# A streaming encoder step: 32 frames of the fifth dense tile move from the all-expert path to gathered rows

## The chip, the core and the metric

One core of a Trainium2 chip runs the whole program. The metric is the device time of one execution in microseconds (us), the median of several runs. TensorE is called PE here (PEld is its weight load), VectorE is DVE, ScalarE is ACT, GpSimd is POOL, and SP is the queue from which most DMAs are issued.

## What is computed

One layer over 1,024 prompt frames and 32 sample frames of width 1,024: an input projection, a differential attention and a recurrent branch, an output projection, and then PEER, a layer of 16,384 single-neuron experts, followed by a last RMSNorm. The change touches PEER and that norm alone:

```python
q = (xs @ w_q).reshape(P_TBLOCK, P_HEADS, 2, P_DQ)
s = einsum('thcd,hckd->thck', q, sub_keys)
sv, si = top_k(s, 16)                              # per half key
cv, ci = top_k(comb, 16)                           # 16 experts of each of 8 heads
e = ...                                            # 128 expert numbers of a frame
gate = softmax(cv)
hid = gelu(einsum('thkd,td->thk', down[e], xs))
out = einsum('thkd,thk->td', up[e], gate * hid)
h = h + out;  y = rmsnorm(h, final_norm)
```

Each frame uses 128 of the 16,384 experts.

## The kernel before

The frames lie in tiles of 128: prompt tiles 0 to 7, and tile S with the 32 sample frames. Five generators (`gemm`, `attn`, `routing`, `scatter`, `rows`) are interleaved by costs that the code gives them; the framework then fixes one order of instructions for each engine when the program is built.

PEER has two forms. **The dense form** (tiles 0 to 4, `DENSE`, together `NV` = 640 frames) sends every frame through all experts. The experts stand as 128 columns of 128. For a column `e`, `hidden(e)` multiplies all frames by the column's down weights (two halves of 320 frames, 24 matmuls each, since each float product is made of three float32r ones) and applies gelu. `gated(e)` multiplies by a gate matrix that is zero nearly everywhere and splits the product into a high and a low part (`vwh`, `vwl`, `WR` = 6 buffers each). Four columns make a block: 32 of them. In a block, the loop over `db` multiplies by the up weights and DVE adds the result to `acc` (L1274). A block has 384 matmuls, half of them of `hidden` for the block that follows. The weights come by `dr` and `ur` (8 loads of 256 KB of each per block).

The gate matrix is made by `scatter()`: four frames at a time, ACT, DVE and POOL build one-hot rows, `grid` multiplies them on PE and evicts them into `stg` (one buffer); every 16 frames one store of 1 MB goes to `W_d` in HBM, from which `gated` loads it (`gw`). The dense stage begins only when all gates are stored. Until then `v_start` makes the first `GE` = 6 columns of gelu values and keeps them in `early`.

**The row form** (`ROWS` = 5, 6, S, 7) gathers. For each of a frame's 128 experts, POOL issues an indirect DMA (L1044) that brings 128 rows of 8 KB (down and up) into one of `RB` = 5 buffers; DVE makes the dot product (L1047, an accumulating multiply), ACT gelu and gate (L1049, L1050), and DVE adds the weighted up row to an accumulator in PSUM (L1031). Only then is the buffer free. Tile S has 32 frames, so its 128 experts are laid in four runs of 32 over the partitions: 32 gathers serve it. At its end the four runs are folded together (L1066 to L1071). Each tile ends with `normed` (L1004) and takes row buffers for that too. That makes 3 x 128 + 32 = 416 gathers.

`routing()` makes the lists (`topk`) on DVE; those of tiles 5, 6, S and 7 are made while the dense stage runs. Work of `rows` is held back in the order of DVE so that it runs at most 60 us of its own cost account ahead of `gemm`.

Of the kernel before, what the change touches and what calls it, by code (L numbers as in the profile page):

```python
# [17 lines left out]
DEC = 32  # L18
# [11 lines left out]
CDG = [[0, 1, 2], [3, 4], [5, 6, 7, "S"]]  # L30

DENSE = [0, 1, 2, 3, 4]
ROWS = [5, 6, "S", 7]
RORDER = [0, 1, 2, 3, 4, 5, 6, 7, "S"]

DEFER = [6, 7]
# [6 lines left out]

PRE = [2, 1]

RB, VR, VB, BB, OHB = 5, 3, 2, 4, 4

CSH = 2

GX = (3, 6, 3)  # L50

GE = 6

GC, SC = 1.65, 1.0

# [4 lines left out]

def rows_of(t):
    return DEC if t == "S" else 128


@with_exitstack
def step_kernel(ctx, tc, x_prompt, x_sample, cache_kT, cache_v, state, norm1, w_in, lam_params,
# [4 lines left out]
    V, A, PE, G, SP = nc.vector, nc.scalar, nc.tensor, nc.gpsimd, nc.sync  # L71
# [46 lines left out]
    ident = consts.tile([128, 128], F32, name="ident")  # L118
# [160 lines left out]
    def halves(x):  # L279
        return x[:, 0:4], x[:, 4:8]  # L280
# [637 lines left out]
    def topk(t):  # L918
        pk, twk = P["pk"], P["twk"]
        T = rows_of(t)  # L920
# [7 lines left out]
        for h0 in range(0, PH, hg):  # L928
# [54 lines left out]
            V.tensor_copy(out=e3[:T, h0:h0 + hg], in_=ef[:T])  # L983
            HEADS[t] = h0 + hg
            yield 1.0
        if t == "S":

            es = pk.tile([128, 32], I32, name="es", tag="es")
            gs = pk.tile([128, 32], F32, name="gts", tag="gts")
            for g in range(4):  # L990
                SP.dma_start(out=es[g * 32:(g + 1) * 32], in_=ei[:32, g * 32:(g + 1) * 32])
                SP.dma_start(out=gs[g * 32:(g + 1) * 32], in_=gate[:32, g * 32:(g + 1) * 32])
            ei, gate = es, gs
        ROUTE[t] = ROUTING[t] = (gate, ei)
        yield 3.0


    def normed(pool, ht, fnb, t, sq):

        T = rows_of(t)  # L1000
        ss = pool.tile([128, 1], F32, name="ssf", tag="ssf", bufs=2)
        A.activation(sq[:T], ht[:T], AF.Square, accum_out=ss[:T])
        r = rstd_of(pool, ss, 1, D, T, tag="f")
        V.scalar_tensor_tensor(out=sq[:T], in0=ht[:T], scalar=r[:T], in1=fnb[:T],  # L1004
                               op0=OP.mult, op1=OP.mult)
        SP.dma_start(out=y_sample if t == "S" else y_prompt[t * 128:t * 128 + 128, :], in_=sq[:T])

    def rows():

        for t in ROWS:  # L1010
            while t not in ROUTING or "gat" not in P:
                yield None
            gate, ei = ROUTING[t]
            T = rows_of(t)
            nk = 32 if t == "S" else 128
            gat = P["gat"]

            def wide(name):
                return gat.tile([128, 2 * D], F32, name=name, tag="row", bufs=RB)

            xt = gat.tile([128, D], F32, name="xg", tag="xg", bufs=1)
            for g in range(128 // T):
                SP.dma_start(out=xt[g * T:(g + 1) * T], in_=xn_d[t][:, :])
            hid = gat.tile([128, 128], F32, name="hid", tag="hid", bufs=1)
            acc = P["xgp"].tile([128, D], F32, name="xp", tag="xp")

            def add(k, row):
                if k == 0 and t == "S":
                    V.tensor_scalar(acc, row[:, D:], hid[:, 0:1], None, op0=OP.mult)
                else:  # L1030
                    V.scalar_tensor_tensor(out=acc, in0=row[:, D:], scalar=hid[:, k:k + 1],  # L1031
                                           in1=acc if k else first, op0=OP.mult, op1=OP.add)

            first = None
            if t != "S":
                first = wide("first")[:, 0:D]
                SP.dma_start(out=first, in_=h1_d[t][:, :])

            late = []
            for k in range(nk):  # L1040
                while t not in ROUTE and HEADS.get(t, 0) * 16 <= k:
                    yield None
                row = wide("row")
                G.indirect_dma_start(out=row, out_offset=None, in_=p_rows,  # L1044
                                     in_offset=bass.IndirectOffsetOnAxis(ap=ei[:, k:k + 1], axis=0))
                h = hid[:, k:k + 1]
                V.tensor_tensor_reduce(out=row[:, 0:D], in0=row[:, 0:D], in1=xt, scale=1.0, scalar=0.0,  # L1047
                                       op0=OP.mult, op1=OP.add, accum_out=h)
# [12 lines left out]
            ht = acc  # L1061
            if t == "S":

                ht = hw[:, 0:D]
                SP.dma_start(out=ht[:T], in_=h1_d[t][:, :])
                V.tensor_copy(out=full, in_=acc)  # L1066
                pw = wide("runs")
                V.tensor_add(ht[:T], ht[:T], acc[:T])
                for g, part in enumerate((pw[:, 0:D], pw[:, D:], sq)):
                    SP.dma_start(out=part[:T], in_=full[(g + 1) * T:(g + 2) * T])  # L1070
                    V.tensor_add(ht[:T], ht[:T], part[:T])  # L1071
            normed(gat, ht, fnb, t, sq)
            yield 4.0


    NV = 128 * len(DENSE)
    SB = 16
    W_d = dram([128 // JB, 128, NV // SB, JB, SB], "W_d")

# [10 lines left out]
    def grid(t, s0, q, stg, am, bm):  # L1090
        ps = ws_bank()
        for u in range(4):
            PE.matmul(ps[:, u * 128:(u + 1) * 128], am[:, u], bm[:, u], start=True, stop=True)  # L1093
        A.activation(stg[:, :, :, q:q + 4],
                     ps.rearrange("p (t b j) -> p b j t", t=4, j=JB), AF.Copy)
        if q + 4 == SB:
            o = (128 * DENSE.index(t) + s0) // SB
            SP.dma_start(out=W_d[:, :, o].rearrange("b i j t -> i b j t"), in_=stg)

    def scatter():  # L1100

        late = None
        for t in [x for ts in CDG for x in ts if x in DENSE]:
# [13 lines left out]
            A.activation(tr[:, 0:3], ps.rearrange("p (a t) -> p a t", a=4)[:, 0:3], AF.Copy)  # L1117
            A.activation(tr[:, 3], ps[:, 0:128], AF.Copy, scale=-1.0)

            for s0 in range(0, 128, SB):  # L1120
                stg = sct.tile([128, 128 // JB, JB, SB], F32, name="stg", tag="stg", bufs=1)
                for q in range(0, SB, 4):
                    pool, bufs = (P["oh"], OHB) if "oh" in P else (sct, 2)
# [19 lines left out]
            late = None  # L1143
            DONE.add(t)

    JU, WR = 4, 6
    NCH = -(-NV // 512)
    CHUNK = NV // NCH
    CS = [slice(j * CHUNK, (j + 1) * CHUNK) for j in range(NCH)]
# [22 lines left out]
    def v_start():  # L1172


        VX["early"] = P["vk"].tile([128, KD, NV], F32, name="early", tag="acc")
        xh = VX["xh"] = P["vx"].tile([128, KD, NV], F32R, name="vxh")
        xl = VX["xl"] = P["vx"].tile([128, KD, NV], F32R, name="vxl")

        places = [(t, i) for t in range(len(DENSE)) for i in range(2)]
        half = len(places) // 2  # L1180
        xs = []
        for h in range(2):
            x = P["gw"].tile([128, half, 512], F32, name="vxs", tag="gw", bufs=2)
            for j, (t, i) in enumerate(places[h * half:(h + 1) * half]):
                SP.dma_start(out=x[:, j], in_=xn_d[DENSE[t]][:, i * 512:(i + 1) * 512])
                xs.append(x[:, j])
        for (t, i), x in zip(places, xs):
            transposed_half(gv_bank, x, 128, halves(xh)[i], halves(xl)[i], 128 * t)
            yield 1.0
        for e in range(GE):  # L1190
            hidden(e)
            yield 3 * KD * NV / 2400.

    def stage_v():
        n = NV
        with tc.tile_pool(name="v_wk", bufs=2) as wk:
# [32 lines left out]
            def residual(d0):  # L1229

                cs = slice(d0 * 128, d0 * 128 + 512)
                for i in range(len(DENSE)):
                    ps = gv_bank()
                    for d in range(4):
                        PE.transpose(ps[:, d * 128:(d + 1) * 128],
                                     acc[:, d0 + d, i * 128:(i + 1) * 128], ident)
                    V.tensor_add(ht[:, i, cs], ht[:, i, cs], ps)
                    A.activation(sq[:, i, cs], ht[:, i, cs], AF.Square,
                                 accum_out=s2[:, d0 // 4, i:i + 1])
                    G.tensor_tensor(out=ht[:, i, cs], in0=ht[:, i, cs], in1=fnb[:, cs], op=OP.mult)  # L1240

            for jb in range(NJ):
                if jb == NJ - 1:
# [2 lines left out]
                    fnb = P["gw"].tile([128, D], F32, name="fnb", tag="gw", bufs=2)  # L1246
                    s2 = wk.tile([128, 2, len(DENSE)], F32, name="s2", tag="s2", bufs=1)
                    ss = wk.tile([128, len(DENSE)], F32, name="ss", tag="ss", bufs=1)
                    late = [(ht[:, i], h1_d[t][:, :]) for i, t in enumerate(DENSE)]
                    late.append((fnb, row_bcast(final_norm)))  # L1250
                for dq in range(4):
                    if jb + 1 < NJ:
# [25 lines left out]

            r = rstd_of(wk, ss, len(DENSE), D, tag="v")
            for i, t in enumerate(DENSE):  # L1280
                V.tensor_scalar(sq[:, i], ht[:, i], r[:, i:i + 1], None, op0=OP.mult)
                SP.dma_start(out=y_prompt[t * 128:t * 128 + 128, :], in_=sq[:, i])
            yield 10.0

    STATE = set()
# [162 lines left out]
```

## Time and profile before

| | |
|---|---|
| median of 3 runs | 3603.99 us (3594.76 to 3604.02) |
| the profiled execution | 3604.3 us |
| its span | 3602.5 us |
| PE, PEld busy | 3259.8 us (90%), 3135.7 us (87%) |
| DVE busy | 2834.6 us (79%) |
| POOL, ACT busy | 2018.5 us (56%), 1614.2 us (45%) |
| mean granted clock of PE | 0.952 |
| DMA | 881.01 MB, mean 245 GB/s |

Busy time is the union of the instructions' times on an engine, and matmuls are pipelined: the spacing of their starts tells their cost, not their duration. What an engine waited for is inferred from semaphores. The granted clock is 1.00 at 2.4 GHz and 0.50 at 1.2 GHz.

### The profile page before, as it was taken

What the parts mean: (1) busy time and instruction counts of PE and PEld (TensorE: products, weight loads), DVE (VectorE), ACT (ScalarE), POOL (GpSimd) and SP (SyncE); (2) the same over time, 40 slices, a digit from 0 to 9 for tenths busy, and PEclk for the clock granted to TensorE, in tenths of its full rate; (3) what the DMA queues carried; (4) which work ended last, traced back from release to release, by engine and by line L of the source; (5) the groups of instructions that cost most, each with busy time, mean ns of one, the idle gap of its engine ahead of it and who ended that gap; (6) DMA issues with size and microseconds to landing.
All of it is one profiled execution on the core that took longest, in us unless ns stands there. A gap on an engine that the chain in (4) does not pass through costs nothing.

```text
span 3602.5 us, 60487 instructions
## 1 busy us (share of the span) xinstructions
PE 3259.8 (90%) x21635; PEld 3135.7 (87%) x21635; DVE 2834.6 (79%) x6148; ACT 1614.2 (45%) x4034; POOL 2018.5 (56%) x1339
## 2 busy tenths in 40 slices
PE   7999899989988888774899888999999999999997
PEld 6989899877877887774899888999999999999997
DVE  3354468898678999988999999888888888788833
ACT  3544344456777747763333333333333333333322
POOL 2322224546334556565666569666766676677633
PEclk9999999999988999886999999999999999999999
DMA  4554364444565635489888778999889898999832
GB/s 163 167 159 149 109 206 167 158 138 149 173 191 161 227 123 153 139 321 343 307 318 323 299 269 312 356 338 359 314 324 355 300 355 324 346 336 351 298 109 94
DMA packets 357453, 881.01 MB, mean 245 GB/s; under 512 B 31008, under 2 KB 190240, under 8 KB 299808
## 3 DMA queue, kind: packets, MB, share of 16 engines
q1 hardware_dynamic: 297248, 440.91, 36.9%
q0 software_dynamic: 59904, 436.23, 31.8%
q8 instruction: 171, 2.80, 0.3%
q14 instruction: 130, 1.06, 0.1%
HBM read 784.47 MB, written 92.14 MB: 243 GB/s over the span
## 4 chain that ended last, share of the span: by engine, by line
PE 57%; DVE 28%; DMA 4%; issue 4%; ACT 3%; POOL 2%; SPq 0%; DVEq 0%; ACTq 0%; POOLq 0%
PE gv L261 12%; PE gv L262 11%; PE gv L263 11%; PE gm L261 6%; PE gm L263 6%; PE gm L262 6%; DVE row L1047 5%; DVE xp L1031 5%; DVE acc L1274 2%; DVE oh L967 2%; PE ws L1093 1%; DVE ohB L1132 1%; DVE ef L972 1%; PE gb L468 1%; DMA row<-in_p_rows_dram,ei 1%
## 5 line engine op out<-in xcount | busy, mean ns | idle before, releaser
L261 PE MATMUL gv<-vwh,uh 128*128 128x320 f32 x2048 | 648.3, 317 | 96.7 <-DVE acc L1274 63.9
L255 POOL TENSOR_TENSOR wl<-wr,wh 128x1024 fp32r<-128x1024 f32 x160 | 390.4, 2453 | 540.7 <-ACT wh L254 524.9
L261 PE MATMUL gv<-vxh,dh 128*128 128x320 f32 x2048 | 643.9, 315 | 21.7 <-DVE acc L1274 10.2
L1044 POOL DMA_INDIRECT row<-in_p_rows_dram,ei x384 | 514.3, 1339 | 259.1 <-DVE xp L1031 141.7
L263 PE MATMUL gv<-vxh,dl 128*128 128x320 f32 x2048 | 639.8, 313 | 8.7 <-POOL dl L255 8.7
L262 PE MATMUL gv<-vwl,uh 128*128 128x320 f32 x2048 | 640.8, 313 | 0.0
L262 PE MATMUL gv<-vxl,dh 128*128 128x320 f32 x2048 | 639.7, 313 | 0.0
L263 PE MATMUL gv<-vwh,ul 128*128 128x320 f32 x2048 | 638.3, 313 | 0.5 <-POOL ul L255 0.5
L1047 DVE CUSTOM_DVE_ANT_0 row<-row,xg 128x1024 f32<-128x1024 f32 x416 | 599.4, 1441 | 3.1 <-DMA row<-in_p_rows_dram,ei 2.1
L1031 DVE SCALAR_TENSOR_TENSOR xp<-row,hid,xp 128x1024 f32<-128x1024 f32 x412 | 528.4, 1283 | 78.8 <-ACT hid L1050 77.0
L261 PEld LDWEIGHTS gv<-vwh,uh 128*128 128x128 f32 x2048 | 391.9, 191 | 111.6 <-DVE acc L1274 76.7
L255 POOL TENSOR_TENSOR dl<-dr,dh 128x512 fp32r<-128x512 f32 x256 | 361.3, 1415 | 201.4 <-ACT dh L254 193.4
L255 POOL TENSOR_TENSOR ul<-ur,uh 128x512 fp32r<-128x512 f32 x256 | 368.0, 1438 | 181.6 <-ACT uh L254 162.3
L261 PEld LDWEIGHTS gv<-vxh,dh 128*128 128x128 f32 x2048 | 392.0, 191 | 28.2 <-DVE vwl L255 13.1
L263 PEld LDWEIGHTS gv<-vxh,dl 128*128 128x128 f32 x2048 | 391.5, 191 | 9.5 <-POOL dl L255 9.5
L262 PEld LDWEIGHTS gv<-vwl,uh 128*128 128x128 f32 x2048 | 392.5, 192 | 0.0
L263 PEld LDWEIGHTS gv<-vwh,ul 128*128 128x128 f32 x2048 | 391.5, 192 | 0.9 <-POOL ul L255 0.9
L262 PEld LDWEIGHTS gv<-vxl,dh 128*128 128x128 f32 x2048 | 392.1, 191 | 0.0
L1135 POOL TENSOR_TENSOR ohB<-ohB,tr 128x512 f32<-128x512 f32 x160 | 200.0, 1256 | 262.4 <-DVE ohB L1132 216.8
L1274 DVE TENSOR_TENSOR acc<-acc,gv 128x320 f32<-128x320 f32 x496 | 235.4, 479 | 93.5 <-PE gv L263 90.2
L1049 ACT ACTIVATE hid<-hid 128x1 f32<-128x1 f32 x416 | 82.9, 199 | 486.5 <-DVE hid L1047 482.1
L254 ACT ACTIVATE uh<-ur 128x512 fp32r<-128x512 f32 x256 | 161.2, 630 | 301.3 <-PE gv L262 209.3
(324 smaller groups left out, 7520.7 us busy)
## 6 DMA issues: line engine op xcount, KB each, us to landing
dr<-in_p_downT_dram SPq DMA_DIRECT2D x256, 256.0 KB
ur<-in_p_up_dram SPq DMA_DIRECT2D x256, 256.0 KB
wr<-in_w_in_dram SPq DMA_DIRECT2D x88, 512.0 KB
W_d<-stg SPq DMA_DIRECT2D x40, 1024.0 KB
gw<-W_d SPq DMA_DIRECT2D x32, 1280.0 KB
wr<-in_p_wq_dram SPq DMA_DIRECT2D x48, 512.0 KB
wr<-in_w_out_dram SPq DMA_DIRECT2D x24, 512.0 KB
wr<-in_w_a_dram SPq DMA_DIRECT2D x12, 512.0 KB
```

What stands on the lines that cost most here:

```text
L254: A.activation(h, src, AF.Copy)
L255: (lo_engine or G).tensor_tensor(out=l, in0=src, in1=h.bitcast(F32), op=OP.subtract)
L261: PE.matmul(out, lh, rh, start=(i == 0), stop=False)
L262: PE.matmul(out, lh, rl, start=False, stop=False)
L263: PE.matmul(out, ll, rh, start=False, stop=(i == n - 1))
L967: V.tensor_tensor(out=oh[:T], in0=cf[:T, h].unsqueeze(2).to_broadcast([T, 16, NCAND]), in1=iota_c[:T].unsqueeze(1).to_broadcast([T, 16, NC ...
L1031: V.scalar_tensor_tensor(out=acc, in0=row[:, D:], scalar=hid[:, k:k + 1], in1=acc if k else first, op0=OP.mult, op1=OP.add)
L1044: G.indirect_dma_start(out=row, out_offset=None, in_=p_rows, in_offset=bass.IndirectOffsetOnAxis(ap=ei[:, k:k + 1], axis=0))
L1047: V.tensor_tensor_reduce(out=row[:, 0:D], in0=row[:, 0:D], in1=xt, scale=1.0, scalar=0.0, op0=OP.mult, op1=OP.add, accum_out=h)
L1049: A.activation(h, h, AF.Gelu)
L1135: G.tensor_tensor(out=bm, in0=bm, op=OP.mult, in1=tr[:, 2, xs].unsqueeze(2).to_broadcast([128, 4, 128]))
L1274: V.tensor_add(acc[:, db, cs], acc[:, db, cs], ps[:, :CHUNK])
```

## The change

Tile 4 is cut: its first 96 frames stay dense, and its last 32 become a row tile "4b" that is handled as S is, ahead of tile 5. The dense form then has 608 frames in two halves of 304, and the scatter of tile 4 ends after 96 frames. There are 448 gathers. `GE` goes from 6 to 8, `WR` from 6 to 8, and `RB` from 5 to 4. The dense norm's reads and writes shrink to the frames that are there.

```diff
 DENSE = [0, 1, 2, 3, 4]
-ROWS = [5, 6, "S", 7]
+CUT = {4: 96}
+ROWS = ["4b", 5, 6, "S", 7]
-RB, VR, VB, BB, OHB = 5, 3, 2, 4, 4
+RB, VR, VB, BB, OHB = 4, 3, 2, 4, 4
-GE = 6
+GE = 8
+def dense_of(t):
+    return CUT.get(t, 128)
...
-        if t == "S":
-            es = pk.tile([128, 32], I32, name="es", tag="es")
-            gs = pk.tile([128, 32], F32, name="gts", tag="gts")
+        if t == "S" or t in CUT:
+            es = pk.tile([128, 32], I32, name="es", tag="es", bufs=2)
+            gs = pk.tile([128, 32], F32, name="gts", tag="gts", bufs=2)
+            o = CUT.get(t, 0)
             for g in range(4):
-                SP.dma_start(out=es[g * 32:(g + 1) * 32], in_=ei[:32, g * 32:(g + 1) * 32])
+                SP.dma_start(out=es[g * 32:(g + 1) * 32], in_=ei[o:o + 32, g * 32:(g + 1) * 32])
...
+            small = t in ("S", "4b")
+            T, of, o = (DEC, 4, CUT[4]) if t == "4b" else (rows_of(t), t, 0)
+            nk = 32 if small else 128
...
-    NV = 128 * len(DENSE)
+    VT = [dense_of(t) for t in DENSE]
+    VO = [sum(VT[:i]) for i in range(len(VT))]
+    NV = sum(VT)
...
-            for s0 in range(0, 128, SB):
+            for s0 in range(0, dense_of(t), SB):
...
-    JU, WR = 4, 6
+    JU, WR = 4, 8
...
-                for i in range(len(DENSE)):
+                for i, (o, T) in enumerate(zip(VO, VT)):
...
+                    V.memset(s2, 1.0)
```

## Rows read from the trace of the kernel before

**Rows 1.** Busy time by stretch: length, PE, PEld, DVE, ACT, POOL; clock; DMA share; GB/s.
```profile
1500.00:1630.00 130.00, 97.50 (x602) 93.05 (x601) 116.55 (x246) 89.50 (x244) 87.70 (x68) 0.84 0.86 304
1630.00:1680.00 50.00, 5.98 (x34) 5.48 (x33) 37.34 (x53) 15.09 (x50) 22.90 (x16) 0.57 0.97 369
1680.00:2290.00 610.00, 546.07 (x3473) 535.96 (x3474) 597.03 (x1272) 214.23 (x572) 424.99 (x296) 0.93 0.84 309
2290.00:3425.00 1135.00, 1112.87 (x7504) 1103.21 (x7503) 941.64 (x1426) 422.92 (x1142) 783.83 (x565) 1.00 0.89 332
3425.00:3603.00 178.00, 156.12 (x1068) 154.82 (x1066) 62.13 (x131) 46.43 (x99) 64.30 (x50) 0.95 0.30 102
```

**Rows 2.** The same view for line L1031 alone: DVE's additions of gathered rows.
```profile
1500.00:1680.00 180.00, 42.17 (x32) 0.77 0.89 322
1680.00:2290.00 610.00, 161.81 (x127) 0.93 0.84 309
2290.00:3425.00 1135.00, 330.32 (x257) 1.00 0.89 332
```

**Rows 3.** Timeline of PE, starts in us: nine of 320 columns, eight of 256.
```profile
2304.80 0.31 PE L261 MATMUL gv<-vxh,dh 128*128 128x320 f32 x1
...
2305.97 0.31 PE L263 MATMUL gv<-vxh,dl 128*128 128x320 f32 x1
...
1011.77 0.28 PE L262 MATMUL gm<-act,wh 128*128 128x256 f32 x1
...
1012.59 0.28 PE L263 MATMUL gm<-act,wl 128*128 128x256 f32 x1
```

**Rows 4.** Groups of instructions: one of six dense groups (busy, mean ns, idle before).
```profile
L261 PE MATMUL gv<-vxh,dh 128*128 128x320 f32 x2048 | 643.9, 315 | 21.7 <-DVE acc L1274 10.2 <-DVE vwl L255 8.6 <-DVE vxl L272 1.9
```

**Rows 5.** The chain that ended last, 1630 to 1682 us: start, length, what.
```profile
1630.70 16.81 DMA W_d<-stg
...
1652.93 1.29 DVE xp L1031
...
1662.00 1.29 DVE xp L1031
...
1678.25 3.48 DVE early L1211 x6
```

**Rows 6.** Stores of the gate matrix, 1500 to 1720 us: count, first and last issue.
```profile
L1098 SPq DMA_DIRECT2D W_d<-stg x8: 370/377/392, 1505.5 to 1652.7; - x8
```

**Rows 7.** Groups of DVE's instructions, 2300 to 3400 us.
```profile
L1047 DVE CUSTOM_DVE_ANT_0 row<-row,xg 128x1024 f32<-128x1024 f32 x249 | 345.5, 1388 | 1.0 <-DMA row<-in_p_rows_dram,es 0.8
L1031 DVE SCALAR_TENSOR_TENSOR xp<-row,hid,xp 128x1024 f32<-128x1024 f32 x247 | 317.7, 1286 | 61.7 <-ACT hid L1050 60.8 <-ACT hid L1049 0.5 <-issue 0.2
```

**Rows 8.** Waits of POOL, 2300 to 3400 us: us in total, times, longest.
```profile
POOL row L1044 <- DVE xp L1031: 85.0, 82, 4.1
```

**Rows 9.** The page's DMA queue of the gathers, and issues with their sizes.
```profile
q0 software_dynamic: 59904, 436.23, 31.8%
...
dr<-in_p_downT_dram SPq DMA_DIRECT2D x256, 256.0 KB
ur<-in_p_up_dram SPq DMA_DIRECT2D x256, 256.0 KB
...
gw<-W_d SPq DMA_DIRECT2D x32, 1280.0 KB
```

**Rows 10.** Timeline of DVE: last row of tile S, first row of tile 7.
```profile
2847.72 1.22 DVE L1047 CUSTOM_DVE_ANT_0 row<-row,xg 128x1024 f32<-128x1024 f32 x1
...
2869.04 1.23 DVE L1047 CUSTOM_DVE_ANT_0 row<-row,xg 128x1024 f32<-128x1024 f32 x1
```

**Rows 11.** Timeline of DVE: the last gathered row, its norm, the last dense addition.
```profile
3421.30 1.22 DVE L1047 CUSTOM_DVE_ANT_0 row<-row,xg 128x1024 f32<-128x1024 f32 x1
...
3430.56 1.27 DVE L1004 SCALAR_TENSOR_TENSOR ht<-xp,rsf,fnb 128x1024 f32<-128x1024 f32 x1
...
3581.58 0.49 DVE L1274 TENSOR_TENSOR acc<-acc,gv 128x320 f32<-128x320 f32 x1 [1.27 <-PE gv L263]
```

More of the change, by code (lines that the diff above doesn't have):

```diff
@@ L985, in topk, with normed @@
             yield 1.0
-        if t == "S":
-            es = pk.tile([128, 32], I32, name="es", tag="es")
-            gs = pk.tile([128, 32], F32, name="gts", tag="gts")
+        if t == "S" or t in CUT:
+            es = pk.tile([128, 32], I32, name="es", tag="es", bufs=2)
+            gs = pk.tile([128, 32], F32, name="gts", tag="gts", bufs=2)
+            o = CUT.get(t, 0)
             for g in range(4):
-                SP.dma_start(out=es[g * 32:(g + 1) * 32], in_=ei[:32, g * 32:(g + 1) * 32])
-                SP.dma_start(out=gs[g * 32:(g + 1) * 32], in_=gate[:32, g * 32:(g + 1) * 32])
-            ei, gate = es, gs
-        ROUTE[t] = ROUTING[t] = (gate, ei)
+                SP.dma_start(out=es[g * 32:(g + 1) * 32], in_=ei[o:o + 32, g * 32:(g + 1) * 32])
+                SP.dma_start(out=gs[g * 32:(g + 1) * 32], in_=gate[o:o + 32, g * 32:(g + 1) * 32])
+            small = "%sb" % t if t in CUT else t
+            ROUTE[small] = ROUTING[small] = (gs, es)
+        if t != "S":
+            ROUTE[t] = ROUTING[t] = (gate, ei)
         yield 3.0
-    def normed(pool, ht, fnb, t, sq):
-        T = rows_of(t)
+    def normed(pool, ht, fnb, dst, sq):
+        T = dst.shape[0]
         ss = pool.tile([128, 1], F32, name="ssf", tag="ssf", bufs=2)
@@ L1005, in normed @@
                                op0=OP.mult, op1=OP.mult)
-        SP.dma_start(out=y_sample if t == "S" else y_prompt[t * 128:t * 128 + 128, :], in_=sq[:T])
+        SP.dma_start(out=dst, in_=sq[:T])
     def rows():
@@ L1013, in rows @@
             gate, ei = ROUTING[t]
-            T = rows_of(t)
-            nk = 32 if t == "S" else 128
+            small = t in ("S", "4b")
+            T, of, o = (DEC, 4, CUT[4]) if t == "4b" else (rows_of(t), t, 0)
+            nk = 32 if small else 128
+            dst = y_sample if t == "S" else y_prompt[of * 128 + o:of * 128 + o + T, :]
             gat = P["gat"]
@@ L1022, in rows @@
             for g in range(128 // T):
-                SP.dma_start(out=xt[g * T:(g + 1) * T], in_=xn_d[t][:, :])
+                SP.dma_start(out=xt[g * T:(g + 1) * T], in_=xn_d[of][o:o + T, :])
             hid = gat.tile([128, 128], F32, name="hid", tag="hid", bufs=1)
@@ L1027, in add @@
             def add(k, row):
-                if k == 0 and t == "S":
+                if k == 0 and small:
                     V.tensor_scalar(acc, row[:, D:], hid[:, 0:1], None, op0=OP.mult)
@@ L1034, in rows @@
             first = None
-            if t != "S":
+            if not small:
                 first = wide("first")[:, 0:D]
@@ L1061, in rows @@
             ht = acc
-            if t == "S":
+            if small:
                 ht = hw[:, 0:D]
-                SP.dma_start(out=ht[:T], in_=h1_d[t][:, :])
+                SP.dma_start(out=ht[:T], in_=h1_d[of][o:o + T, :])
                 V.tensor_copy(out=full, in_=acc)
@@ L1071, in rows @@
                     V.tensor_add(ht[:T], ht[:T], part[:T])
-            normed(gat, ht, fnb, t, sq)
+            normed(gat, ht, fnb, dst, sq)
             yield 4.0
-    NV = 128 * len(DENSE)
+    VT = [dense_of(t) for t in DENSE]
+    VO = [sum(VT[:i]) for i in range(len(VT))]
+    NV = sum(VT)
     SB = 16
@@ L1096, in grid @@
         if q + 4 == SB:
-            o = (128 * DENSE.index(t) + s0) // SB
+            o = (VO[DENSE.index(t)] + s0) // SB
             SP.dma_start(out=W_d[:, :, o].rearrange("b i j t -> i b j t"), in_=stg)
@@ L1184, in v_start @@
             for j, (t, i) in enumerate(places[h * half:(h + 1) * half]):
-                SP.dma_start(out=x[:, j], in_=xn_d[DENSE[t]][:, i * 512:(i + 1) * 512])
+                SP.dma_start(out=x[:VT[t], j], in_=xn_d[DENSE[t]][:VT[t], i * 512:(i + 1) * 512])
                 xs.append(x[:, j])
         for (t, i), x in zip(places, xs):
-            transposed_half(gv_bank, x, 128, halves(xh)[i], halves(xl)[i], 128 * t)
+            transposed_half(gv_bank, x, VT[t], halves(xh)[i], halves(xl)[i], VO[t])
             yield 1.0
@@ L1231, in residual @@
                 cs = slice(d0 * 128, d0 * 128 + 512)
-                for i in range(len(DENSE)):
+                for i, (o, T) in enumerate(zip(VO, VT)):
                     ps = gv_bank()
                     for d in range(4):
[L1235 to L1240, printed above, removed]
+                        PE.transpose(ps[:T, d * 128:(d + 1) * 128], acc[:, d0 + d, o:o + T], ident)
+                    V.tensor_add(ht[:T, i, cs], ht[:T, i, cs], ps[:T])
+                    A.activation(sq[:T, i, cs], ht[:T, i, cs], AF.Square,
+                                 accum_out=s2[:T, d0 // 4, i:i + 1])
+                    G.tensor_tensor(out=ht[:T, i, cs], in0=ht[:T, i, cs], in1=fnb[:T, cs], op=OP.mult)
             for jb in range(NJ):
@@ L1248, in stage_v @@
                     ss = wk.tile([128, len(DENSE)], F32, name="ss", tag="ss", bufs=1)
-                    late = [(ht[:, i], h1_d[t][:, :]) for i, t in enumerate(DENSE)]
+                    V.memset(s2, 1.0)
+                    late = [(ht[:VT[i], i], h1_d[t][:VT[i], :]) for i, t in enumerate(DENSE)]
                     late.append((fnb, row_bcast(final_norm)))
@@ L1280, in stage_v @@
             for i, t in enumerate(DENSE):
-                V.tensor_scalar(sq[:, i], ht[:, i], r[:, i:i + 1], None, op0=OP.mult)
-                SP.dma_start(out=y_prompt[t * 128:t * 128 + 128, :], in_=sq[:, i])
+                T = VT[i]
+                V.tensor_scalar(sq[:T, i], ht[:T, i], r[:T, i:i + 1], None, op0=OP.mult)
+                SP.dma_start(out=y_prompt[t * 128:t * 128 + T, :], in_=sq[:T, i])
             yield 10.0
```

## The prediction

> **What bounds the kernel now.** I first read busy time by stretch, because the share over the whole span mixes stages. From 1500 us on there are four of them [rows 1]. Up to 1680 us the gate matrix is finished: in the last 50 us of that PE works 6 us. From 1680 to 2290 us DVE is busy 597 of 610 us: it makes the lists of the later tiles, takes gathered rows and serves the dense loop. From 2290 to 3425 us PE is busy 1112.9 of 1135 us at a granted clock of 1.00 (2.4 GHz), with DVE at 83%: here PE sets the pace of the dense loop. From 3425 us to the end PE runs alone with few transfers (102 GB/s).
>
> There is a second stream beside PE: the rows. Their last dot product starts at 3421.3 us, 160 us before the dense loop's last addition at 3581.6 us [rows 11]. So the dense path ends last today, and the rows have 160 us of room. The question is whether that room holds when 32 gathers are added and the dense path gets shorter.
>
> What sets the pace of the rows? Between 2290 and 3425 us 257 rows were added [rows 2], 4.42 us each. One gather is 436.23 MB / 416 = 1.049 MB [rows 9]. PE issued 7504 matmuls, so 19.54 blocks of 384, 58.1 us each. A block loads 8 `dr`, 8 `ur` (0.262 MB each) and one `gw` (1.311 MB) [rows 9], together 5.51 MB. With 257 / 19.54 = 13.15 rows that is 19.3 MB per block, or 332 GB/s: exactly the rate that the stretch shows [rows 1], at a DMA share of 0.89. I read this as rows filling what the weights leave of the DMA engines. DVE hardly ever waited for a landing (1.0 us in 249 rows [rows 7]), while POOL waited 85.0 us for the release of a buffer [rows 8]: the rows stand landed in their buffers and wait for their turn in DVE's order, which was fixed when the program was built.
>
> **The change, part by part.** *Narrower matmuls.* The starts are 1.17 us / 8 = 146 ns apart at 320 columns and 0.82 / 7 = 117 ns at 256 [rows 3]: 0.455 ns per column, so 304 columns cost 139 ns, 7.2 ns less. There are 6 x 2048 = 12,288 of them [rows 4]. In the PE-bound stretch 7504 x 7.2 = 54 us go, in the last one some 1030 x 7.2 = 7 us. In the DVE-bound stretch 3473 x 7.2 = 25 us are on offer, and I count nothing of it here, since DVE has 13 us of idle time there. The page "TensorE: Matmul & The Clock Gate" of the Trainium skill, section "Back-to-back issue gap", gives about 81 ns at 128 columns and 131 ns at 512 for a sustained stream; by that slope (0.13 ns per column, an estimate) the two terms together would be 18 us, not 61. The trace disagrees with the level already (146 ns at 320), so its own slope stands.
>
> *The shorter scatter.* Tile 4 makes all eight of the stores between 1505.5 and 1652.7 us [rows 6], 21 us apart; two go, which is 42 us off the wait for the last one (16.8 us for the store before it [rows 5]). PE's idle stretch at 1630 us could shrink by 0 to 42 us. What follows is DVE-bound, so what counts is DVE's idle time that can be filled: 12.7 us in the 50 us up to 1680 and 13.5 us before [rows 1]. I take 25 us and keep 0 and 42 for the range.
>
> *Eight early columns, eight buffers.* Two more `hidden` (96 matmuls, 14 us) move into the idle stretch. That pays only where PE binds behind it, so I take 0 of 0 to 14. Two more `vwh`/`vwl` buffers could remove PE's wait for `vwl`, 8.6 us at one of six groups [rows 4]; I take 0 of 0 to 9.
>
> *DVE.* 32 rows at 1.39 + 0.08 (reading the accumulator) + 1.29 us are 88 us [rows 7], and a fold of about 10. They fit into 193 us of idle time between 2290 and 3425 and 116 us after it [rows 1]; without that cover they would cost 98 us.
>
> *Queues.* 16 small DMAs or so for the list, the frames and the fold pass SP; at 0.377 us per issue, the one row of an SP issue that I read [rows 6], that is 6 us, ahead of weight loads that are three buffers deep. I take 0 of 0 to 6. The copies of the list wait for `topk` of tile 4; behind them in SP stand weight loads only.
>
> *Dense path.* 3602.5 - 25 - 54 - 7 = 3516.5 us of span, its last matmul at about 3581 - 86 = 3495 us.
>
> *Rows path.* A new block takes 58.1 - 384 x 0.0072 = 55.3 us. At 332 GB/s it moves 18.36 MB, of which the weights and the smaller gates take 5.44: 12.3 rows remain, 4.49 us each. By 2290 us 32 + 127 = 159 rows were done [rows 2]. In the new kernel that point lies 25 us earlier (5 rows less), two stores of 1 MB are gone (2 more), and the end of 4b costs a pause: from the last row of S to the first of tile 7 pass 21.3 us instead of 4.4 [rows 10], 17 us or 4 rows. So 152. The remaining (7504 + 1068) / 384 = 22.3 blocks bring 22.3 x 12.3 = 275, and the last block, without `dr` and `gw`, 3 more: 430. Of 448 rows 18 are left when the last dense matmul ends. Alone they run at the pace that the chain shows between 1652.93 and 1662.00 us, three rows in 9.07 us, 3.02 us each [rows 5]: 54 us, so 3549 us. Then the norm of the last tile (3430.56 + 1.27 - 3422.52 = 9.3 us [rows 11]) and the store (6.5 us, as from the dense norm's last instruction to the end): 3565 us of span. The profiled execution took 1.8 us more than its span: **3567 us**. That execution (3604.3 us) is 0.3 us above the median, so no correction. The end passes from the dense path to the rows, which eat 49 of the 86 us.
>
> *Four row buffers* are the unknown. No row of this trace has four. From below: today five buffers hold a row for 5 x 4.42 = 22 us. The transfer takes 31.8% of 3602.5 us / 416 = 2.75 us of all 16 engines [rows 9], DVE 2.76 us; with issue and ACT that stays under 9 us, so four buffers allow a row every 2.2 us, and the cost is 0. From above: if the 22 us are needed as they are, four allow one in 5.5 us, which is 22.3 x 2.2 = 49 rows fewer in the blocks, 148 us. I take 0, since DVE waited only 1.0 us for landings, so that most of the 22 us is standing.
>
> **Rivals.** *The dense path ends last: 3518 us, chance 0.20.* It needs 13.1 rows in a block of 55.3 us, which is 346 GB/s. For it: 369 GB/s between 1630 and 1680 us [rows 1]. Against it: 332 over 1135 us. The page "DMA: Bandwidth & Descriptors", section "Specifications", names about 358 GB/s of HBM per core as the limit; the 369 of that short stretch lies above, the 332 below, and by 358 (an estimate) 13.7 rows would fit, which speaks for this rival.
>
> *Four buffers starve the rows: 3649 us, chance 0.22.* The place is POOL's gather, which waits for the addition four rows back [rows 8]. With 10% fewer rows, 11.1 per block, 27 more are left: 82 us. It decides from 11.8 rows per block on (4.7 us per row): then 12 more rows at 3.02 us use up the 37 us gained. For it: POOL waits for buffers already with five, and each tile's end takes two of them, a small tile's three of four. Against it: the landings above.
>
> *Narrower matmuls are not cheaper: 3579 us, chance 0.10.* If spacing doesn't follow the columns, blocks stay at 58.1 us, 13.2 rows fit in each, the rows end with the dense path, and only the scatter's 25 us are left. Against it: [rows 3].
>
> **How the numbers follow.** The forecast itself has 0.42 (3530 to 3600), and 0.06 is for what I don't see, half of it slower. What can be told from no change is 0.3%, so 3593 to 3615 us counts as the same. Faster: 0.33 of the forecast, the 0.20, 0.08 of the matmul case, 0.02 of the unseen: 0.63. Same: 0.07 of the forecast, 0.02 of the matmul case, 0.03 of the starving rows, 0.01 of the unseen: 0.13. Slower: 0.19 of the starving rows, 0.02 of the forecast, 0.03 of the unseen: 0.24. The range goes from 3512 (the dense path with a little more of the scatter) to 3640 (most of the starving case, up to 9% fewer rows).
>
> **What would show it.** Right: starts of 304-column matmuls about 139 ns apart; the first dense addition some 30 us earlier; blocks of about 55 us after 2290; DVE with rows until about 3545 us, and the last instructions `normed` of tile 7, behind the dense norm; rows alone about 3 us apart. Wrong: if PE's work ends last, DMA carried more than 340 GB/s; if rows fall under 11.8 per block with POOL waiting for L1031 and DVE for landings, it is the buffers; if the spacing stays at 146 ns, it is the matmul.

## The result and the profile after

The changed kernel took 3632.22 us, median of five runs (3625.15 to 3645.12), against 3603.99 us: a ratio of 1.0084 with a 95% interval of [1.0059, 1.0110]. It is slower by 0.8%, where 3567 us and a faster kernel were forecast. The execution profiled took 3627.32 us, of which 3625.6 us are its span.

The same view as [rows 1], of the changed kernel (length; PE, PEld, DVE, ACT, POOL; clock; DMA share; GB/s):

```profile
1500.00:1630.00 130.00, 96.12 (x607) 90.09 (x605) 113.06 (x220) 78.44 (x212) 80.15 (x62) 0.87 0.90 317
1630.00:1680.00 50.00, 42.46 (x281) 41.09 (x282) 45.75 (x130) 22.57 (x62) 33.49 (x23) 0.93 0.84 320
1680.00:2290.00 610.00, 554.62 (x3776) 547.21 (x3775) 593.94 (x1191) 209.62 (x552) 415.45 (x294) 0.96 0.78 283
2290.00:3425.00 1135.00, 1105.48 (x7914) 1102.29 (x7912) 959.85 (x1439) 430.97 (x1155) 762.80 (x578) 0.99 0.89 328
3425.00:3626.00 201.00, 0.00 (x0) 0.00 (x0) 165.38 (x226) 33.44 (x132) 91.69 (x63) 0.50 0.91 351
```

And that of [rows 2], the rows' additions alone (now L1043), with the tail:

```profile
1680.00:2290.00 610.00, 143.97 (x113) 0.96 0.78 283
2290.00:3425.00 1135.00, 308.77 (x240) 0.99 0.89 328
3425.00:3626.00 201.00, 84.92 (x66) 0.50 0.91 351
```

PE's work is gone from the last stretch: the dense path has become much shorter. But 66 rows are added there, and only 113 were added between 1680 and 2290 us, where the kernel before had 127 with 32 rows fewer to do in all. The timeline of DVE at the end answers to [rows 11]: the last dense addition, the last gathered row's addition, the norm of its tile:

```profile
3410.48 0.46 DVE L1288 TENSOR_TENSOR acc<-acc,gv 128x304 f32<-128x304 f32 x1
...
3615.59 1.29 DVE L1043 SCALAR_TENSOR_TENSOR xp<-row,hid,xp 128x1024 f32<-128x1024 f32 x1 [0.60 <-ACT hid L1062]
...
3620.37 1.28 DVE L1013 SCALAR_TENSOR_TENSOR ht<-xp,rsf,fnb 128x1024 f32<-128x1024 f32 x1
```

In the kernel before the last row's addition was this one:

```profile
3423.13 1.29 DVE L1031 SCALAR_TENSOR_TENSOR xp<-row,hid,xp 128x1024 f32<-128x1024 f32 x1 [0.60 <-ACT hid L1050]
```

The dense path ends 171 us earlier than before (3411 against 3582 us), and the last row's addition comes 192 us later (3616 against 3423 us). Counted in the same view from 3412 us on, 69 rows stand behind the last dense addition; they take 205 us, 2.97 us each. The forecast had 18 rows there.

Two groups of the page, DVE's dot product and POOL's gathers, with the idle time before them:

```profile
L1059 DVE CUSTOM_DVE_ANT_0 row<-row,xg 128x1024 f32<-128x1024 f32 x448 | 708.8, 1584 | 26.7 <-DMA row<-in_p_rows_dram,ei 26.6
L1056 POOL DMA_INDIRECT row<-in_p_rows_dram,ei x384 | 510.8, 1330 | 333.2 <-DVE xp L1043 228.7
```

POOL now stands 228.7 us for the release of a buffer and DVE 26.6 us for landings; in the kernel before the same two groups showed 141.7 and 3.1 us. Both say "buffers", but 26.6 us alone are far from the 65 us between forecast and result.

Starts of PE, to answer [rows 3], twelve intervals of 304 columns:

```profile
2704.62 0.30 PE L267 MATMUL gv<-vxh,dh 128*128 128x304 f32 x1
...
2706.29 0.30 PE L267 MATMUL gv<-vxh,dh 128*128 128x304 f32 x1
```

1.67 us / 12 = 139 ns, as forecast.

### The profile page after: what moved, and what is told of

It reads as the page before. It is cut to its first block, busy times and chain, and to the rows that moved or that the text cites. A ratio compares the mean times of both kernels' runs of the same rounds, so it can differ in the third digit from the quotient of the medians.

```text
span 3625.6 us, 60544 instructions
## 1 busy us (share of the span) xinstructions
PE 3147.6 (87%) x21571; PEld 3033.1 (84%) x21571; DVE 2965.3 (82%) x6255; ACT 1602.7 (44%) x4052; POOL 2023.6 (56%) x1363
## 4 chain that ended last, share of the span: by engine, by line
PE 52%; DVE 28%; DMA 7%; issue 6%; POOL 4%; ACT 2%; SPq 0%; POOLq 0%; DVEq 0%; ACTq 0%
PE gv L267 10%; PE gv L269 10%; PE gv L268 10%; PE gm L267 6%; PE gm L269 6%; PE gm L268 6%; DVE row L1059 5%; DVE xp L1043 4%; DMA ur<-in_p_up_dram 2%; DVE oh L973 2%; DVE ohB L1146 2%; POOL row L1056 1%; DVE ef L978 1%; DMA row<-in_p_rows_dram,ei 1%; PE ws L1107 1%
## 5 line engine op out<-in xcount | busy, mean ns | idle before, releaser
L1059 DVE CUSTOM_DVE_ANT_0 row<-row,xg 128x1024 f32<-128x1024 f32 x448 | 708.8, 1584 | 26.7 <-DMA row<-in_p_rows_dram,ei 26.6
L1056 POOL DMA_INDIRECT row<-in_p_rows_dram,ei x384 | 510.8, 1330 | 333.2 <-DVE xp L1043 228.7
L267 PE MATMUL gv<-vxh,dh 128*128 128x304 f32 x2048 | 633.1, 309 | 55.7 <-DVE vwl L261 34.7
L1043 DVE SCALAR_TENSOR_TENSOR xp<-row,hid,xp 128x1024 f32<-128x1024 f32 x443 | 568.1, 1282 | 99.9 <-ACT hid L1062 98.3
L267 PE MATMUL gv<-vwh,uh 128*128 128x304 f32 x2048 | 622.4, 304 | 19.7 <-ACT uh L260 15.1
L269 PE MATMUL gv<-vxh,dl 128*128 128x304 f32 x2048 | 626.3, 307 | 11.9 <-POOL dl L261 11.9
L268 PE MATMUL gv<-vxl,dh 128*128 128x304 f32 x2048 | 628.0, 307 | 0.0
L268 PE MATMUL gv<-vwl,uh 128*128 128x304 f32 x2048 | 619.5, 303 | 4.2 <-DVE vwl L261 4.2
L269 PE MATMUL gv<-vwh,ul 128*128 128x304 f32 x2048 | 617.6, 303 | 0.9 <-POOL ul L261 0.9
L261 POOL TENSOR_TENSOR ul<-ur,uh 128x512 fp32r<-128x512 f32 x256 | 349.3, 1365 | 178.8 <-ACT uh L260 159.3
L267 PE MATMUL gm<-xh,wh 128*128 128x320 f32 (+1 forms) x768 | 252.3, 329 | 0.0
```

The costliest lines, as they stand in the source:

```text
L261: (lo_engine or G).tensor_tensor(out=l, in0=src, in1=h.bitcast(F32), op=OP.subtract)
L267: PE.matmul(out, lh, rh, start=(i == 0), stop=False)
L268: PE.matmul(out, lh, rl, start=False, stop=False)
L269: PE.matmul(out, ll, rh, start=False, stop=(i == n - 1))
L1056: G.indirect_dma_start(out=row, out_offset=None, in_=p_rows, in_offset=bass.IndirectOffsetOnAxis(ap=ei[:, k:k + 1], axis=0))
```

## The experiments

Each edit is told against the changed kernel, unless it says otherwise; `RB` is the number of row buffers, `WR` that of `vwh`/`vwl` buffers, `GE` that of early columns. The kernel before gave 3604 to 3606 us beside them, and ratios are to it. I begin with the cut by itself.

### The cut alone, with five row buffers

```diff
-RB, VR, VB, BB, OHB = 4, 3, 2, 4, 4
+RB, VR, VB, BB, OHB = 5, 3, 2, 4, 4
-GE = 8
+GE = 6
-    JU, WR = 4, 8
+    JU, WR = 4, 6
```

> The cut of tile 4 alone, with five row buffers, six vwh/vwl buffers and six early columns as before. Theory A (the rows end last; they get what the weights leave, and the small ring of four buffers is one cause of their being late, the early end of the dense path the other): blocks of about 55 us, some 27 rows stand behind the last dense addition in the order of DVE where the changed kernel has 68, so 27 x 3.05 us = 82 us behind a dense loop that ends near 3460: about 3560 us. Theory B (four buffers alone make the loss): also near 3560, and the run with four buffers and six vwh buffers goes back to 3630. Theory C (32 more rows cost more than narrower matmuls give, whatever the buffers): 3620 us or more.

Measured: 3559.06 us (3557.75 to 3570.07), 0.9878 [0.9842, 0.9914]. The cut is a gain of 1.2%, and the 3567 us forecast came near it, though two of its terms missed by some 30 us each way (see below). The last dense addition, of the `acc` group, starts at 3461 us:

```profile
3461.41 0.46 DVE L1288 TENSOR_TENSOR acc<-acc,gv 128x304 f32<-128x304 f32 x1
```

What makes the changed kernel slow is in the three sizes that were changed with it.

### The same with four row buffers

```diff
-GE = 8
+GE = 6
-    JU, WR = 4, 8
+    JU, WR = 4, 6
```

> The cut with four row buffers, but six vwh/vwl buffers and six early columns. Theory A: 39 rows behind the last dense addition, 12 more than with five buffers: 12 x 3.05 = 37 us later than the cut alone, about 3595 us. Theory B: all of the loss is here, 3625 us or more. Theory C: as the changed kernel, 3620 to 3640.

Measured: 3611.26 us (3601.42 to 3619.21), 1.0014 [0.9998, 1.0030]: between theory A (3595) and theory B (3625 or more). One buffer of five costs 52 us and with it the whole gain. To see where, the stretches of both. First five buffers, all engines up to 2290 us and from there to 3400 us, in the columns of [rows 1]:

```profile
1680.00:2290.00 610.00, 554.63 (x3778) 544.98 (x3778) 597.27 (x1219) 224.80 (x592) 458.48 (x312) 0.96 0.87 321
2290.00:3400.00 1110.00, 1084.19 (x7693) 1075.45 (x7692) 929.55 (x1410) 418.45 (x1137) 761.20 (x569) 1.00 0.91 336
```

and its rows:

```profile
1500.00:1680.00 180.00, 39.77 (x31) 0.83 0.88 313
1680.00:2290.00 610.00, 165.32 (x129) 0.96 0.87 321
2290.00:3400.00 1110.00, 315.17 (x245) 1.00 0.91 336
```

Then four buffers, the same two views:

```profile
1680.00:2290.00 610.00, 544.75 (x3570) 534.44 (x3571) 572.75 (x1171) 211.91 (x557) 427.07 (x294) 0.91 0.82 297
2290.00:3400.00 1110.00, 1089.32 (x7728) 1080.96 (x7727) 941.61 (x1418) 422.83 (x1137) 753.31 (x565) 1.00 0.91 335
```

```profile
1500.00:1680.00 180.00, 34.59 (x27) 0.84 0.84 294
1680.00:2290.00 610.00, 151.84 (x119) 0.91 0.82 297
2290.00:3400.00 1110.00, 312.37 (x243) 1.00 0.91 335
```

After 2290 us the two are alike: two rows and 1 GB/s. The loss lies before: 14 rows (4 of them ahead of 1680 us), 208 matmuls, and from 1680 to 2290 us 24.5 us more of idle time on DVE, the engine that is the bound there. PE's granted clock in that stretch is 0.91 instead of 0.96, with 153 instead of 147 ns of busy time per matmul, so part of the missing matmuls is a slower PE. At the end 28 rows stand behind the last dense addition with five buffers and 40 with four; 12 rows at 3.0 us are 36 us, and the last dense addition itself comes 21 us later:

```profile
3482.59 0.46 DVE L1288 TENSOR_TENSOR acc<-acc,gv 128x304 f32<-128x304 f32 x1
```

Together 57 us, against 61 us between the two spans (3556.4 and 3617.3; the execution profiled with four buffers is the slowest of its ten, 8 us above the median).

### Four row buffers without the cut

An edit of the kernel before:

```diff
-RB, VR, VB, BB, OHB = 5, 3, 2, 4, 4
+RB, VR, VB, BB, OHB = 4, 3, 2, 4, 4
```

> The kernel before with four row buffers and nothing else changed: what the ring alone costs where the dense path ends last. Theory A: the rows end some 30 us later than at 3422 us, still inside the 160 us of room, so 3604 us within 0.3%. Theory B: rows 10% slower or more end behind 3580 us, and the time rises over 3620 us.

Measured: 3584.80 us (3578.29 to 3599.50), 0.9943 [0.9927, 0.9960], a gain, where I expected 3604. The rows are held back here too (the dot product that started at 2127 us starts at 2161, and the last addition of a row comes at 3461 instead of 3423 us), but they have 160 us of room, and the dense loop gets DVE: its last addition moves from 3582 to 3561 us. So one and the same edit costs 52 us where rows end last and gives 20 us where the dense path does.

### Is it the 32 frames?

The changed kernel, and the cut alone, each without the row tile 4b:

```diff
-ROWS = ["4b", 5, 6, "S", 7]
+ROWS = [5, 6, "S", 7]
```

> The changed kernel without the row tile 4b: the last 32 frames of tile 4 are left out of PEER and of the last norm, so this leaves work out. Theory A: rows still end last, 32 of them behind the last dense addition where there were 68, so 36 x 3.05 = 110 us less than the changed kernel: about 3520 us. Theory C: the same or less. If the time stays over 3580 us, the rows of 4b aren't what the end waits for.

> The cut alone (five row buffers, six vwh/vwl buffers, six early columns) without the row tile 4b: its 32 frames are left out of PEER and of the last norm. This measures the dense path's gain by itself. Theory A: no row stands behind the last dense addition, the dense path ends last, with its last addition near 3455 us and a tail of 20 us as before: 3480 us, where the forecast's own sum for the dense path was 3518. If the time is 3510 or more, the gain of the dense path in the cut was over-read.

Measured: 3504.14 us (0.9715 [0.9683, 0.9747]) for the changed kernel without 4b, and 3492.74 us (0.9694 [0.9678, 0.9710]) for the cut alone without it (expected: about 3520 and 3480). In the first the rows still end last, 102 us behind the dense additions (3492 and 3390 us), although they are 416 as before: a kernel with these three sizes has them late even without more of them. In the second the dense path ends last (additions 3468 us, rows 3451 us). That is what the shorter dense path gives by itself, by narrower matmuls and by the shorter scatter: 3606 - 3493 = 113 us, where I had 86. Putting the 32 rows back costs 66 us with five row buffers and 128 us with the sizes of the change.

### A smaller cut

The cut alone (first diff) with 112 dense frames and 16 gathered in eight runs, halves of 320 and 304 columns, and then with four row buffers. The lines that take the widths of the halves and the size of the small tile from these are left out here:

```diff
-CUT = {4: 96}
+CUT = {4: 112}
...
-    CHUNK = NV // NCH
-    CS = [slice(j * CHUNK, (j + 1) * CHUNK) for j in range(NCH)]
+    CS = [slice(0, 320), slice(320, NV)]
...
```

> Half the cut: 112 frames of tile 4 stay dense, 16 gather in eight runs of 16 (16 gathers); halves of 320 and 304 frames; five row buffers, six vwh/vwl buffers, six early columns. Theory A (both paths end near each other when half as much is moved): blocks of about 56.2 us (half the matmuls at 146, half at 139 ns), dense loop's last addition near 3520 us, one row behind it in DVE's order; about 3545 us, 0.4% under the cut of 32 (3559). If the time is 3560 or more, the rows are late for another reason than their number.

> Half the cut with four row buffers. Theory A: the ring costs rows between 1500 and 2290 us and none later; 11 rows stand behind the last dense addition, which comes some 15 us earlier (3505 us) because DVE is left to it: 3505 + 11 x 3.05 + 17 = 3556 us, 10 us more than with five buffers, where the cut of 32 lost 52.

Measured: 3568.24 us (0.9900 [0.9883, 0.9917]) and 3589.19 us (0.9953 [0.9935, 0.9972]). With 16 frames both paths end together (last dense addition 3540, last row's 3550 us), but the times lie 23 and 33 us above the 3545 and 3556 that I had expected: the dense loops end at 3540 and 3533 us, not at 3520 and 3505. The ring costs 21 us here, two fifths of its price with 32 frames. Rows end last by 10 us with five buffers and by 46 us with four; that the price depends on how far the rows end behind fits these two cuts and isn't tried further.

### Half of each gather

The cut alone, and each gather brings the 4 KB of the down row only. The table in HBM then holds no up rows, and the addition reads the down half again; those lines are left out here:

```diff
-                G.indirect_dma_start(out=row, out_offset=None, in_=p_rows,
+                G.indirect_dma_start(out=row[:, 0:D], out_offset=None, in_=p_rows,
...
```

> The cut alone, but each gather brings the down half of a row only (4 KB of 8); DVE multiplies and adds as before, with wrong values: the up rows are left out. Theory A (rows get what the weights leave of the DMA engines): 15 to 17 rows per block wherever DVE has time, the rows end some 150 us before the dense loop, and the time falls to the dense path's, 3485 us. If DVE's order or its own time sets the pace of the rows, 3550 us or more.

Measured: 3623.37 us (3612.01 to 3628.56), 1.0052 [1.0038, 1.0065]. I had expected 3485: half the bytes made it slower by 64 us than the cut alone. Its stretch and its rows from 2290 to 3400 us:

```profile
2290.00:3400.00 1110.00, 1002.16 (x6817) 989.60 (x6815) 947.66 (x1493) 401.51 (x1107) 769.18 (x561) 0.94 0.66 218
2290.00:3400.00 1110.00, 342.59 (x268) 0.94 0.66 218
```

What PE waited for in it, here and in the cut alone:

```profile
PE gv L267 <- DVE acc L1288: 84.4, 26, 8.6
...
PE gv L267 <- DVE acc L1288: 22.5, 21, 2.1
```

DVE's dot products in it with their idle time, here and in the cut alone:

```profile
L1059 DVE CUSTOM_DVE_ANT_0 row<-row,xg 128x1024 f32<-128x1024 f32 x268 | 364.5, 1378 | 39.2 <-DMA row<-in_p_rows_dram,ei 35.7 <-DMA row<-in_p_rows_dram,es 3.1
...
L1059 DVE CUSTOM_DVE_ANT_0 row<-row,xg 128x1024 f32<-128x1024 f32 x246 | 360.6, 1466 | 0.2
```

The count of rows per block came out as theory A had it: 268 / (6817 / 384) = 15.1 instead of 12.2. But most of that is a longer block (62.5 instead of 55.4 us); in the same 1110 us 268 rows were added instead of 245, 9% more for half the bytes. And the run doesn't show that bytes had held the rows back on the chip, because its order of DVE is another one: some 264 rows stand ahead of the 240th dense addition, 223 in the cut alone. That order asks for rows earlier than they land: DVE waits 38.8 us for landings of half the size, where the cut alone shows 0.2 us of idle time before its dot products. PE waits 84.4 us for DVE's additions, and its granted clock is 0.94 instead of 1.00 (147 instead of 141 ns of busy time per matmul). The rows' last addition ends at 3441 us and the dense path at 3599 us. What the run does show is that rows placed earlier in DVE's order are paid for by the dense loop. Whether DMA or the built order sets the pace of the rows in the cut stays open.

### Eight buffers, and eight columns

Four row buffers and eight `vwh`/`vwl` buffers, with six early columns:

```diff
-GE = 8
+GE = 6
```

> The changed kernel with six early columns instead of eight (four row buffers, eight vwh/vwl buffers). In DVE's order 68 rows stand behind the last dense addition, as with eight early columns. Theory A: 3630 us, so the 20 us between four buffers alone (3611) and the changed kernel come from the eight vwh/vwl buffers, which make the dense path faster at the rows' expense; the early columns give nothing. Theory D (the early columns cost it): 3611 us.

Measured: 3619.55 us (3616.66 to 3628.88), 1.0042 [1.0027, 1.0056], 8 us above the kernel with six buffers, where 3630 was expected. The two ratios' intervals just touch (1.0014 [0.9998, 1.0030]), and the chips were two. The dense path gains 87 us by the two buffers (last addition at 3396 instead of 3483 us). None of it reaches the end: 69 rows stand behind it instead of 40.

The changed kernel, with eight columns, lay 13 us above. The two hadn't been timed side by side, so both ran once more, on one chip:

> The changed kernel with six early columns instead of eight (four row buffers, eight vwh/vwl buffers), beside the changed kernel itself on the same chip. Theory A, the two columns cost about 0.4%: their 96 matmuls and their ACT work stand in the stretch up to 1680 us ahead of dense work and rows alike, and rows end last; then this one is 10 to 15 us faster than the changed kernel, some 3619 against 3632 us. Theory B, the 13 us between the two medians seen so far lie between two chips: then both give the same time within 4 us, somewhere from 3620 to 3632 us.

> The changed kernel itself on the chip of e11_wr8_ge6. Theory A, the early columns cost: 3632 us, ratio 1.008 to the kernel before and 10 to 15 us above e11. Theory B, the chip: the same as e11 within 4 us. In both its rows end last, about 3615 us, and the last dense addition lies at about 3411 us.

Measured: 3618.19 us (3617.20 to 3625.07), 1.0040 [1.0027, 1.0053], and for the changed kernel 3630.08 us (3619.12 to 3637.66), 1.0069 [1.0050, 1.0088]. So the two early columns do cost some 12 us, though the two intervals touch. The last dense addition comes at 3412 us with eight and 3400 us with six, and 72 rows instead of 70 follow after 3400 us. Which of the 96 matmuls, of ACT's gelus or of the loads ahead of them delays the rest wasn't tried.

### Three row buffers

The kernel with the cut and four row buffers, with one less:

```diff
-RB, VR, VB, BB, OHB = 4, 3, 2, 4, 4
+RB, VR, VB, BB, OHB = 3, 3, 2, 4, 4
```

> The cut with three row buffers (six vwh/vwl buffers, six early columns). Theory A (the ring sets the rows' pace before 2290 us, where a buffer is held about 20 us, and hardly after): 63 rows stand behind the last dense addition, which comes near 3490 us; alone they take a buffer's life of about 10.8 us / 3 = 3.6 us each: 3490 + 227 + 17 = 3730 us. Fewer rows than with four buffers between 1500 and 2290 us (146 there), nearly as many between 2290 and 3400 (243 there). If the loss spreads evenly over both stretches, the ring binds everywhere.

Measured: 3733.54 us (3715.95 to 3750.18), 1.0372 [1.0339, 1.0404]. The time is the one expected (3730), the place of the loss only in part. Waits of DVE and its rows, 2290 to 3400 us:

```profile
DVE row L1059 <- DMA row<-in_p_rows_dram,ei: 72.4, 66, 4.6
```

```profile
2290.00:3400.00 1110.00, 298.55 (x232) 0.99 0.88 320
```

Here is how a ring looks that binds in the PE-bound stretch too: DVE waits 72.4 us for landings, and 11 rows are missing against four buffers, where theory A had nearly none. The picture that I had looked for in the prediction comes one buffer later than the loss.

## Why the prediction was wrong

**What held.** The cut alone (the forecast's own case, four buffers at 0) took 3559 us, against 3567 forecast. That this is so near is in part luck: the dense loop ended 33 us earlier than forecast (3462 against 3495), and 28 rows instead of 18 stood behind it, 10 x 3.0 = 30 us. The two misses belong together, since a dense loop that ends earlier leaves more rows to the end. The rows end last; 304 columns cost 139 ns; a block takes 1110 / (7693 / 384) = 55.4 us (55.3 forecast) and holds 245 / 20.03 = 12.2 rows (12.3, though the reason given for it, rows filling what the weights leave of the DMA engines, is not shown); alone at the end, rows are 3.0 us apart (3.02); `normed` of tile 7 is the last. Against the rival that needed 13.1 rows in a block, the DMA rate stayed at 336 GB/s. The page "DMA: Bandwidth & Descriptors" of the Trainium skill, section "Specifications", gives about 358 GB/s per core as the limit; alone in the tail of the changed kernel, from 3500 to 3600 us, the gathers moved 372 GB/s, so here it is passed. What held the stretch at 336 isn't shown.

**The step that failed is "Four row buffers", taken at 0.** It measured 52 us with the cut, and with it the whole gain went; the 21 us more that make a loss of it came with the two other sizes. Two things were wrong in it. First, I bounded it from rows of 2290 to 3400 us and applied it to the 22.3 blocks behind; there it is indeed two rows. For the time up to 2290 us I took 152 finished rows without any term for the ring, and there the loss is: 14 rows, 10 of them where DVE is the bound. Second, "DVE waited only 1.0 us for landings, so that most of the 22 us is standing" reads slack out of an order that was written for five buffers. Each engine's order is fixed when the program is built. With four buffers the built order itself puts 40 rows instead of 28 behind the last dense addition (39 and 27 were expected from it before the runs), and DVE's waits for landings, 8.8 us between 1680 and 2290 us, show only a part of it. That no wait is seen in a planned order shows that the plan fits its buffers, not that it can do with fewer. How the builder comes to the later rows wasn't looked into.

DVE's time in that stretch shows the rest. The groups of the dot product between 1680 and 2290 us (count, busy, mean ns, idle before). The cut alone, five buffers:

```profile
L1059 DVE CUSTOM_DVE_ANT_0 row<-row,xg 128x1024 f32<-128x1024 f32 x130 | 194.2, 1493 | 0.0
```

with four:

```profile
L1059 DVE CUSTOM_DVE_ANT_0 row<-row,xg 128x1024 f32<-128x1024 f32 x120 | 192.7, 1606 | 8.8 <-DMA row<-in_p_rows_dram,ei 8.8
```

and the changed kernel:

```profile
L1059 DVE CUSTOM_DVE_ANT_0 row<-row,xg 128x1024 f32<-128x1024 f32 x112 | 202.0, 1804 | 5.1 <-DMA row<-in_p_rows_dram,ei 5.1
```

With four buffers DVE lost 24.5 us to idle time and 120 x 0.113 = 14 us to longer dot products. In the changed kernel it is busy again (593.9 of 610 us), but 112 x 0.311 = 35 us of that are the longer dot products: 16 rows fewer than the cut alone, with hardly more idle time.

**The rival of starving rows** (3649 us, 0.22) gave the sign, and its threshold of 11.8 rows in a block was passed: 235 / (7863 / 384) = 11.5 from 2290 to 3400 us. But it isn't right in its place. By itself the ring leaves 243 / (7728 / 384) = 12.1 there; the rest came with the eight `vwh`/`vwl` buffers. With six early columns that kernel has 235 rows in the 1110 us and 235 / (7773 / 384) = 11.6 in a block:

```profile
2290.00:3400.00 1110.00, 1089.62 (x7773) 1086.50 (x7771) 946.68 (x1409) 420.69 (x1132) 736.77 (x563) 0.99 0.89 326
```

Blocks that come a little faster (54.8 instead of 55.2 us) don't account for it, and neither does a full DMA, which moved 326 GB/s where it had moved 335. The dot products are longer there too (1607 against 1532 ns, 18 us in all); they and the order of DVE are the candidates left, and neither was tried.

**Eight buffers, "0 of 0 to 9", and eight columns, "0 of 0 to 14",** were mis-sized, and by the medians had the wrong sign. I priced the buffers by one wait of PE. They gave the dense path 87 us, by letting the dense loop run ahead in the DVE-bound stretch (3936 matmuls from 1680 to 2290 us in the kernel of the last pair with six columns, 3570 with six buffers), but on DVE's time. The dot products between 1680 and 2290 us took longer in that kernel, 1835 ns each against 1606:

```profile
L1059 DVE CUSTOM_DVE_ANT_0 row<-row,xg 128x1024 f32<-128x1024 f32 x115 | 211.0, 1835 | 1.5 <-DMA row<-in_p_rows_dram,ei 1.5
```

The end was the rows', and it moved some 8 us later. The columns added 12 us more. So a gain to the path that doesn't end last needn't be worth nothing: where both use the same engine, it can be a loss.

**The shorter dense path** was sized too low: its last addition, forecast at about 3495 us, came at 3462 in the cut alone. The first dense addition came 41 us earlier (1701 against 1742 us), the whole of the 42 us of the two stores, of which I had counted 25. And the 25 us of narrower matmuls in the DVE-bound stretch, counted at nothing, were partly had: 156 of the 496 additions were done by 2290 us, against 132. DVE found the time in 10 of the 26 us that it had stood idle between 1500 and 1680 us (16.5 are left), in fewer one-hot rows of the scatter, in a part of the later tiles' lists that now comes ahead of 1680 us (8 of 32 sorts of half keys), and in shorter dot products (1493 against 1568 ns).

**The sum in its own terms.** From the cut alone to the changed kernel, 28 rows behind the last dense addition became 69, 41 x 3.0 = 123 us, and that addition came 51 us earlier: 72 us later in all, against 69 us between the spans. By the medians the 73 us are 52 for the ring, 8 for the eight buffers and 13 for the columns, in this order of steps: neither the eight buffers nor the eight columns were tried with five row buffers.

**A version that beats both** is the cut alone with the old sizes: 3559 us, 1.2% under the kernel before.

## What to carry to other kernels

A ring of buffers has to be checked in every stretch, not only in the longest: here the fifth buffer was worth 14 rows up to 2290 us and 2 rows from there to 3400. The trace of an order that was planned around the larger ring can't show that a smaller one is enough; time it alone. When a change moves work from one stream to another, the other may end last from then on, and buffers or engine time taken from it then cost time, while a speed-up of the first is paid for by it too. Parts that were changed together should be timed apart: here a gain of 1.2% lay under three sizes that cost 2%.

## What the runs showed of the hardware

DVE's dot product, with two inputs from SBUF, doesn't have one duration. In the changed kernel it took 1.22 us in the mean where POOL did nothing beside it (34 of them) or only issued a gather (157); beside POOL's multiplies and subtractions of float tensors (257) it took 1.86 us in the mean and up to 5.88 us. The timeline of DVE and of POOL in the changed kernel:

```profile
2043.33 5.88 DVE L1059 CUSTOM_DVE_ANT_0 row<-row,xg 128x1024 f32<-128x1024 f32 x1
...
3404.42 3.03 DVE L1059 CUSTOM_DVE_ANT_0 row<-row,xg 128x1024 f32<-128x1024 f32 x1
...
3605.88 1.22 DVE L1059 CUSTOM_DVE_ANT_0 row<-row,xg 128x1024 f32<-128x1024 f32 x1
```

```profile
2043.87 1.76 POOL L976 TENSOR_TENSOR oh<-oh,E 128x800 f32<-128x800 f32 x1
2045.58 2.54 POOL L261 TENSOR_TENSOR dl<-dr,dh 128x512 fp32r<-128x512 f32 x2
...
3403.82 2.54 POOL L1253 TENSOR_TENSOR ht<-ht,fnb 128x512 f32<-128x512 f32 x2
3406.52 1.78 POOL L1056 DMA_INDIRECT row<-in_p_rows_dram,ei  x1 [0.16 <-issue]
```

The one of 3.03 us starts within POOL's pair and ends 1.09 us after it (3407.45 against 3406.36 us), about the time of a whole one: it seems to have stood until POOL was done. The one of 5.88 us starts 0.54 us ahead of POOL's first operation and ends 1.09 us after the last of three in a row (2049.21 against 2048.12 us), so starting first didn't help it, as far as POOL's times can be trusted. The page "SBUF — State Buffer" of the Trainium skill, section "Who interferes with whom", says that a DVE instruction with two inputs from SBUF contends with a GpSimd instruction that reads SBUF, and calls the shared port pair an exclusive lock; this trace agrees. It says too that an operation with one SBUF input isn't touched, and the trace agrees there as well: the rows' addition, which has its accumulator in PSUM, took 1.28 us in the mean, and 1.29 at most where one is recorded by itself, beside POOL's work or not. Only the first addition of a tile, which reads its second input from SBUF as well (`first`), took up to 1.64 us. From 1680 to 2290 us the longer dot products make 35 us of DVE, as above. Why the changed kernel's order meets POOL's work more often than that of the cut alone wasn't tried and stays open.

The other surprise is half a gather: taking 118 GB/s off the DMA engines (336 to 218) made the kernel 64 us slower, in an order of DVE that takes rows earlier.
